# Twenty of eighty expert-score classes in three rounded passes instead of one plain fp32 product, their low parts made by GpSimd

## The chip, the cores and the metric

The kernel runs on one core of a Trainium2 chip. The metric is the device time of one execution in microseconds (us), median over runs. Engine names are those of the profile: PE is the matrix engine (TensorE), PEld its weight loads, DVE VectorE, ACT ScalarE, POOL GpSimd, SP the queue that issues direct DMAs.

## The reference, cut to what matters

The model has two layers. Each ends in a PEER expert block over 256 tokens of width 1024, with 16384 experts:

```
s1, s2 = q[..., :half] . k1, q[..., half:] . k2        # 8 heads, 128 keys each
top 16 of s1, top 16 of s2, top 16 of their 256 sums -> idx, gate = softmax(top)
act = gelu(u_tab[idx] . t)                              # per token, head and choice
out = sum (gate * act) * v_tab[idx]
```

A token picks 8 x 16 of the 16384 experts.

## The kernel before, in words

**Two ways to the experts.** The experts are sorted into 128 classes of 128. For the first `X` = 80 classes the kernel works densely: it computes the scores of all 128 experts of a class for all 256 tokens on PE (80 score classes, "S"), multiplies them by a matrix of gates that is zero where a token has not chosen an expert, and multiplies by the class's rows of `v_tab` (80 value classes, "V"). The other experts are gathered row by row with indirect DMAs issued by POOL and worked on DVE (`gather()`).

**One peer block, in order.** `products()` first makes the queries with `wq` (8 heads, each 2 tiles of 512 KB) in three passes, `mm3`: both factors are split into a rounded high part and a remainder, and high x high, high x low and low x high are added up in one bank. For the weights, ACT makes the high part (a cast into a `whl` tile) and POOL or DVE the low part (a subtraction). For the tokens, `hh` and `hl` (tiles `phh` and `phl`) are high and low, `hf` (`phf`) the plain fp32 values; all three exist before and after the change. Then follow the 80 score classes, 8 fp32 products of 128x256 each, which the profile shows as 16 records, and a Gelu by ACT (`ge<-pa`, later `sg<-pa`). The 80 value classes come last.

**Choosing, at the same time, on DVE.** `choose()` runs `stage2(0)` and `stage2(1)` for the two halves of the tokens: sums of candidates, MAX8/MATCH_REPLACE8/FIND_INDEX8 scans, then long f16 tensor_tensor trees that turn positions into expert numbers. `turn(0)` and `turn(1)` are four PE transposes each (`pa<-identb,ge`) of what a half has chosen. `take8` makes the first lists for the gathers, six memsets prepare the `rows` tiles for gathered rows, and `spread()` builds the gate matrix in 32 blocks: one-hots `o`, `eq` and `oc` on DVE, products `pb<-oc,o` on PE. Three of the six `rows` tiles are the three `whl` buffers, two more are `phl` and `phh`.

**The order.** The kernel's program is written out by a planner: `schedule()` advances the generators of PE work and DVE work by a clock of costs (for PE 0.00167 us a column for a plain fp32 product and 0.00042 for a rounded one), and what is emitted stands in that order on each engine's queue. The chip then follows it in order on every engine, with semaphores between them. The planner's costs know nothing of one engine disturbing another.

**Feeding weights.** `Feed` loads tiles with SP into four `wr` buffers, two or more ahead. A tile with an engine letter is split when it is at most two ahead of its use: the cast goes to ACT's queue, the subtraction for "G" to POOL's. A tile with `None` is used as it is. A `whl` buffer can be filled again when PE has read the tile three before. The bound `feed.hold` stops splitting from the point where `rows` takes the `whl` buffers.

Of the kernel before, what the change touches and what calls it, by code (L numbers as in the profile page):

```python
# [22 lines left out]
KD = 8  # L23
# [2 lines left out]

X = 80
GSC = 32768.0
ROOM = 36
TB, TL = 8, 4  # L30
CAP = 50
# [166 lines left out]
def tile_backbone(ctx: ExitStack, tc: tile.TileContext, a: dict, out: bass.AP):  # L198
# [5 lines left out]
    T, V, S, G, Q = (Engine(e, n, clock) for e, n in ((nc.tensor, "T"), (nc.vector, "V"), (nc.scalar, "S"), (nc.gpsimd, "G"), (nc.sync, "D")))  # L204
# [20 lines left out]
    def pa():  # L225
        t = pp.tile([P, 512], F32, tag="pa", name="pa")
        return t
# [22 lines left out]
    def mm(o, lhsT, rhs, start=True, stop=True):  # L250
        T.matmul(o, lhsT, rhs, start=start, stop=stop)

    def mm3(o, lh, ll, rh, rl, start=True, stop=True):
        T.matmul(o, lh, rh, start=start, stop=False)
        T.matmul(o, lh, rl, start=False, stop=False)
        T.matmul(o, ll, rh, start=False, stop=stop)
# [55 lines left out]
    def x_close():  # L312
        xpool.pop().close()
# [84 lines left out]
    PEER = [(w, c_) for w in "SV" for c_ in range(X)]  # L398
    feed = Feed()
# [5 lines left out]
    for l in range(2):  # L405
        if l:
            feed.add([a["gm_w_v"][n, j] for n in range(4) for j in range(4)] + [a["gm_w_u"][n, j] for n in range(8) for j in range(2)]
                     + [a["gm_w_out"][k] for k in range(16)], GENG)
        feed.add([a["wq"][l, h, j] for h in range(8) for j in range(2)])
        feed.add([a[f"dn{l}"][c_, 0 if w == "S" else 1] for w, c_ in PEER], None)  # L410

    def warm(ps, x):

# [999 lines left out]
    def peer(l, mod, a2, sh2):  # L1413
# [20 lines left out]
        hf = q1.tile([P, KD, 256], F32, name="phf", tag="phf")  # L1434
        hl = q1.tile([P, KD, 256], F32R, name="phl", tag="phl")
        hh = q1.tile([P, KD, 256], F32R, name="phh", tag="phh")
# [20 lines left out]
        def token_major():  # L1457
# [10 lines left out]
            x_close()  # L1468
            qr["s"] = qs = Scratch(ge[:, X - ROOM:, :])
            vals.extend(qs.tile([P, 2, 8, 16], F32, name=f"vals{t}") for t in range(2))  # L1470
# [18 lines left out]
        def stage2(t):  # L1489
# [84 lines left out]
            V.tensor_copy(pk[:, 1, :], i1f)  # L1574
            V.tensor_scalar(pk[:, 2, :], gte[t], GSC, None, op0=ALU.mult)
            V.scalar_tensor_tensor(pk[:, 3, :], gte[t], GSC, pk[:, 2, :], op0=ALU.mult, op1=ALU.subtract)
            yield
# [14 lines left out]
        def turn(t):  # L1592
            pt = pa().bitcast(F16)
            for i in range(4):
                T.transpose(pt[:, i * P:(i + 1) * P], pks[t][:, i, :], identb)
            S.copy(pkT[t], pt[:, :4 * P].rearrange("p (a b) -> p a b", a=4))
# [21 lines left out]
        scored, begun, spreaded = [0], [0], [0]  # L1618

        def spread():  # L1620
# [12 lines left out]
            def apply():  # L1633
                t, b, n, ps, _ = pss.pop(0)
                for i in range(NB):
                    t0 = t * P + b * TB + i * TL
                    v = ps[i][:, :TL * X].rearrange("p (j c) -> p c j", c=X)
                    if n < X:
                        S.activation(ge[:, n:X, t0:t0 + TL], v[:, n:X, :], AF.Copy, scale=1.0 / GSC)
                    o = ge[:, 0:n, t0:t0 + TL]  # L1640
                    V.scalar_tensor_tensor(o, v[:, 0:n, :], 1.0 / GSC, o, op0=ALU.mult, op1=ALU.mult)
                spreaded[0] = t0 + TL
# [31 lines left out]
        def products():  # L1674
            pend = []

            def flush():
                h, qT = pend.pop(0)
                for t in range(2):
                    pss = pa()  # L1680
                    for f in range(2):
                        mm(pss[:, f * P:(f + 1) * P], qT[:, f * 256 + t * P:f * 256 + (t + 1) * P], k12[:, f, h, :])
                    topk1(t, h, pss)

            for h in range(8):
                ps = [pa() for _ in range(2)]
                for j in range(2):
                    wh, wl = feed.get()
                    for f in range(2):
                        for k in range(4):  # L1690
                            mm3(ps[f][:, :256], wh[:, k, f * P:(f + 1) * P], wl[:, k, f * P:(f + 1) * P], hh[:, 4 * j + k, :], hl[:, 4 * j + k, :],
                                j == 0 and k == 0, j == 1 and k == 3)
                if h == 0:
                    token_major()
                qT = qr["s"].tile([P, 512], F32, tag="qT", name="qT", bufs=2)
                for f in range(2):
                    S.copy(qT[:, f * 256:(f + 1) * 256], ps[f][:, :256])
                pend.append((h, qT))
                if h:
                    flush()  # L1700
                yield
            flush()
            done.add("q")

            pair, late = [], []

            def flush_late():

                while late and late[0][0] <= spreaded[0]:
                    _, g_, s_ = late.pop(0)  # L1710
                    V.tensor_tensor(g_, g_, s_, op=ALU.mult)

            for w, c_ in order:
                left[0] -= 1
                if w == "S":
                    u_ = feed.get()
                    ps = pa()
                    for k in range(KD):
                        mm(ps[:, :256], u_[:, k, :], hf[:, k, :], k == 0, k == KD - 1)
                    if len(late) > 2:  # L1720
                        yield lambda: late[0][0] <= spreaded[0]
                        flush_late()
                    n = begun[0]
                    if n:
                        sg = q2.tile([P, 256], F32, tag="sg", name="sg", bufs=4)
                        S.activation(sg[:, :n], ps[:, :n], AF.Gelu)
                    flush_late()
                    if n:
                        late.append((n, ge[:, c_, :n], sg[:, :n]))
                    if n < 256:  # L1730
                        S.activation(ge[:, c_, n:], ps[:, n:256], AF.Gelu)
                    scored[0] += 1
                    if c_ + 1 == X:
                        done.add("S")
                else:
                    while "G" not in done:
                        yield lambda: "G" in done
                    flush_late()
                    if not py[0][0]:
                        for t in range(2):  # L1740
                            for m in range(2):
                                py[t][m] = pb()
                    if c_ == X - 1:
                        done.add("pl")
                    pair.append((ge[:, c_, :], feed.get(2 if c_ >= X - 2 else 1)))
                    if c_ == X - 2:
                        continue
                    for t in range(2):
                        for m, (g_, v_) in enumerate(pair):
                            for n in range(4):  # L1750

                                mm(py[t][n // 2][:, n % 2 * 256:(n % 2 + 1) * 256], g_[:, t * P:(t + 1) * P], v_[:, 2 * n:2 * n + 2, :],
                                   c_ == 0 and n % 2 == 0, c_ == X - 1 and m == 1 and n % 2 == 1 and "shared" in done)
                    pair.clear()
                    done.add("pv")
                    if c_ == 15:
                        done.add("held")
                yield

        def choose():  # L1760
            wait[0], feed.eager = QWAIT, False
            yield lambda: "q" in done
            wait[0] = GTH
            yield from stage2(0)
            for i, _ in enumerate(stage2(1)):
                if i == 4:
                    turn(0)
                yield
            for r_ in range(EARLY):
                take8(0, r_)  # L1770
                yield
            turn(1)
            feed.hold = True
            qr["2"] = eqr.enter_context(tc.tile_pool(name="qr", bufs=2, side="right"))
            qr["rows"] = [whl(f"rows{i}", F32) for i in range(NWH)]
            qr["rows"] += [q1.tile([P, 2 * D], F32, name=f"rows{NWH + i}", tag=("phl", "phh", "row5")[i]) for i in range(NR - NWH)]
            qr["junk"] = qr["2"].tile([P, D], BF16, name="junk", bufs=1)
            for i, r_ in enumerate(qr["rows"]):
                V.memset(r_, 0.0)
            done.add("sel")  # L1780
            todo_v[:] = [order.index(("V", 0)), 2 * P // TB]
            yield from spread()
            done.add("G")
            todo_v[:] = []
            wait[0] = LAST
# [345 lines left out]
```

## Time and profile before

| | |
|---|---|
| runs (3) | median 2077.2 us, 2073.23 to 2078.44 |
| profiled execution | 2073.34 us, of which span 2071.6 us |
| busy in the span | PE 1945.0, PEld 1574.3, DVE 1368.5, ACT 540.4, POOL 592.2 us |
| granted PE clock, mean | 0.973 |
| HBM read | 525.60 MB |

The profile is of one execution. Busy time is the union of an engine's records; a mean duration of a matmul record is longer than the spacing of two, because matmuls overlap. The first score class begins at 520.0 us in layer 0 and at 1409.5 us in layer 1.

### The profile page before, as it was taken

How to read it: one execution, taken by the hardware profiler on the slowest of the kernel's cores; microseconds unless marked ns; L12 is line 12 of the kernel's file. 1: busy time of each engine (PE TensorE's matmuls, PEld its weight loads, DVE VectorE, ACT ScalarE, POOL GpSimd, SP SyncE). 2: the span in 40 equal slices, each digit the busy share in tenths (PEclk: the TensorE clock that was granted, in tenths of full speed). 3: DMA queues.
4: the chain of work that ended last, by engine and by line, in shares of the span. 5: the costliest groups of instructions: out<-in, count | busy, mean ns of one | idle time of the engine just before them, and what ended most of it. 6: DMA issues, size and time to landing. Idle time of an engine off the chain costs nothing.

```text
span 2071.6 us, 28401 instructions
## 1 busy us (share of the span) xinstructions
PE 1945.0 (94%) x10048; PEld 1574.3 (76%) x10048; DVE 1368.5 (66%) x3634; ACT 540.4 (26%) x1386; POOL 592.2 (29%) x378
## 2 busy tenths in 40 slices
PE   7899999999989999998999998999899999989997
PEld 4565444579878888887877788789688888878786
DVE  3575566247988678878664226579888887776651
ACT  4434343344212122210111154442122221101100
POOL 1324222166011112223221188550111112233210
PEclk9999999999989999999999999999999999989999
DMA  8556664555468668998997364454678788989972
GB/s 302 171 184 215 212 217 145 165 173 184 133 225 293 237 220 310 379 378 293 417 410 260 132 234 153 156 191 128 229 283 307 269 297 298 365 295 412 413 274 82
DMA packets 132489, 519.98 MB, mean 251 GB/s; under 512 B 17222, under 2 KB 17414, under 8 KB 107179
## 3 DMA queue, kind: packets, MB, share of 16 engines
q1 hardware_dynamic: 100320, 312.24, 43.2%
q0 software_dynamic: 30720, 204.69, 25.9%
q8 instruction: 79, 1.29, 0.2%
q10 hardware_dynamic: 1296, 1.15, 0.2%
q14 instruction: 74, 0.61, 0.1%
HBM read 525.60 MB, written 6.91 MB: 257 GB/s over the span
## 4 chain that ended last, share of the span: by engine, by line
PE 55%; DVE 19%; issue 12%; DMA 7%; POOL 5%; ACT 2%; POOLq 0%; SPq 0%; ACTq 0%; DVEq 0%
PE pb L169 28%; PE pa L169 27%; DVE ge L169 6%; DMA wr<-in_dn 4%; POOL rows L169 2%; DVE mk L169 2%; POOL whl L169 2%; DVE acc L169 1%; DVE junk L169 1%; DMA acs<-acc 1%; DVE rows L169 1%; DMA rows<-in_uv,gidx 1%; DVE x L169 1%; DVE oc L169 1%; DVE cacc L169 0%
## 5 line engine op out<-in xcount | busy, mean ns | idle before, releaser
L169 PE MATMUL pa<-phf,wr 128*128 128x256 f32 x2560 | 576.1, 386 | 0.0
L169 PE MATMUL pb<-wr,ge 128*128 128x256 f32 x2560 | 569.4, 383 | 6.5 <-DMA wr<-in_dn 5.4
L169 PEld LDWEIGHTS pb<-wr,ge 128*128 128x128 f32 x2560 | 485.2, 191 | 90.3 <-DMA wr<-in_dn 22.9
L169 PEld LDWEIGHTS pa<-phf,wr 128*128 128x128 f32 x2560 | 492.3, 194 | 67.2
L169 POOL DMA_INDIRECT rows<-in_uv,gidx x200 | 231.7, 1158 | 916.8 <-DVE acc L169 608.0
L169 POOL TENSOR_TENSOR whl<-wr,whl 128x1024 fp32r<-128x1024 f32 (+2 forms) x130 | 314.7, 2434 | 401.9 <-ACT whl L169 392.2
L169 DVE SCALAR_TENSOR_TENSOR junk<-rows,h 128x1024 bf16<-128x1024 f32 x200 | 244.0, 1220 | 85.6 <-DMA rows<-in_uv,gidx 82.5
L169 DVE SCALAR_TENSOR_TENSOR acc<-rows,wt,acc 128x1024 f32<-128x1024 f32 x196 | 250.7, 1279 | 0.0
L169 ACT ACTIVATE act<-act 128x1 f32<-128x1 f32 x206 | 41.7, 203 | 435.6 <-DVE junk L169 420.6
L169 ACT CAST whl<-wr 128x1024 fp32r<-128x1024 f32 (+2 forms) x136 | 136.9, 1018 | 70.7 <-PE pa L169 27.7
L169 ACT ACTIVATE sg<-pa 128x256 f32<-128x256 f32 (+25 forms) x126 | 38.8, 308 | 383.9 <-PE pa L169 375.4
L169 PE MATMUL pb<-oc,o 128*128 128x80 f16 x1024 | 88.2, 255 | 31.8 <-DVE oc L169 31.8
L169 PEld LDWEIGHTS <-o 128*128 128x128 f16 x1024 | 80.8, 118 | 40.9 <-DVE o L169 16.3
L169 PE MATMUL pa<-phh,whl 128*128 128x256 f32 x512 | 96.3, 285 | 2.1 <-DVE phf L169 2.1
L169 PE MATMUL pb<-aw,condT 128*32 128x512 f32 x328 | 93.4, 624 | 5.1 <-DVE mod L169 3.0
L169 DVE SCALAR_TENSOR_TENSOR ge<-pb,ge 128x80 f32<-128x80 f32 (+29 forms) x128 | 36.9, 316 | 78.3 <-ACT ge L169 77.2
L169 PEld LDWEIGHTS pa<-phh,whl 128*128 128x128 f32 x512 | 80.8, 191 | 4.0 <-DVE phf L169 2.5
L169 PE MATMUL pa<-phl,whl 128*128 128x256 f32 x256 | 73.2, 286 | 2.4 <-POOL phl L169 1.3
L169 DVE SCALAR_TENSOR_TENSOR mk<-jp,j,gte 128x128 f32<-128x128 f32 x256 | 72.4, 347 | 1.1
L169 PE MATMUL pb<-whl,cath 128*128 128x512 f32 x192 | 61.8, 400 | 2.0 <-POOL whl L169 1.1
L169 ACT ACTIVATE wt<-act,gsel 128x1 f32<-128x1 f32 x200 | 58.9, 295 | 6.5
L169 DVE TENSOR_TENSOR oc<-eq,pkT 128x640 f16<-128x640 f16 x128 | 57.1, 487 | 2.2
(517 smaller groups left out, 2402.0 us busy)
## 6 DMA issues: line engine op xcount, KB each, us to landing
wr<-in_dn SPq DMA_DIRECT2D x320, 512.0 KB
aw<-in_ada_w SPq DMA_DIRECT2D x164, 256.0 KB
wr<-in_wq SPq DMA_DIRECT2D x32, 512.0 KB
wr<-in_w_out SPq DMA_DIRECT2D x16, 512.0 KB
wr<-in_gm_w_v SPq DMA_DIRECT2D x16, 512.0 KB
wr<-in_gm_w_u SPq DMA_DIRECT2D x16, 512.0 KB
wr<-in_gm_w_out SPq DMA_DIRECT2D x16, 512.0 KB
wr<-in_w_xbc SPq DMA_DIRECT2D x12, 512.0 KB
```

The lines of the kernel that those rows point to most:

```text
L169: return f(*args, **kw)
```

## The change

The first `N3` = 20 score classes of each layer are computed with `mm3`, 24 rounded products in place of 8 fp32 ones. Their tiles go through the feed with the letter "G": a cast on ACT and a subtraction on POOL for each. The 60 other classes stay as they are. `choose()` may not pass the point after `turn(1)` before 20 classes are scored in the planner's order.

```diff
+N3 = 20
...
-        feed.add([a[f"dn{l}"][c_, 0 if w == "S" else 1] for w, c_ in PEER], None)
+        feed.add([a[f"dn{l}"][c_, 0] for _, c_ in PEER[:N3]], "G")
+        feed.add([a[f"dn{l}"][c_, 0 if w == "S" else 1] for w, c_ in PEER[N3:]], None)
...
                     for k in range(KD):
-                        mm(ps[:, :256], u_[:, k, :], hf[:, k, :], k == 0, k == KD - 1)
+                        if c_ < N3:
+                            mm3(ps[:, :256], u_[0][:, k, :], u_[1][:, k, :], hh[:, k, :], hl[:, k, :], k == 0, k == KD - 1)
+                        else:
+                            mm(ps[:, :256], u_[:, k, :], hf[:, k, :], k == 0, k == KD - 1)
...
             turn(1)
+            yield lambda: scored[0] >= N3
             feed.hold = True
```

## Rows read from the trace of the kernel before

**Rows 1.** The page: busy times of the engines, and the chain by engine.
```profile
PE 1945.0 (94%) x10048; PEld 1574.3 (76%) x10048; DVE 1368.5 (66%) x3634; ACT 540.4 (26%) x1386; POOL 592.2 (29%) x378
...
PE 55%; DVE 19%; issue 12%; DMA 7%; POOL 5%; ACT 2%; POOLq 0%; SPq 0%; ACTq 0%; DVEq 0%
```

**Rows 2.** Busy time by stretch: length, PE, PEld, DVE, ACT, POOL, clock, DMA.
```profile
519.90:602.70 82.80, 73.93 (x347) 64.36 (x346) 78.39 (x339) 16.57 (x34) 7.46 (x5) 0.96 0.49 164
602.70:800.00 197.30, 189.14 (x1135) 166.38 (x1135) 151.71 (x358) 41.95 (x193) 27.41 (x26) 0.95 0.71 251
...
865.00:1120.00 255.00, 243.47 (x1105) 207.77 (x1104) 187.30 (x466) 31.48 (x125) 76.98 (x63) 0.98 0.95 369
1120.00:1174.00 54.00, 54.00 (x229) 43.02 (x228) 4.26 (x10) 2.37 (x5) 0.00 (x0) 1.00 0.36 119
...
1409.00:1492.00 83.00, 74.32 (x351) 64.75 (x350) 78.58 (x341) 16.93 (x35) 5.57 (x5) 0.97 0.50 164
```

**Rows 3.** PE in order of time, score classes: start, length, records, wait before.
```profile
520.03 34.70 PE L169 MATMUL pa<-phf,wr 128*128 128x256 f32 x160
...
554.79 24.39 PE L169 MATMUL pa<-phf,wr 128*128 128x256 f32 x112
579.37 0.82 PE L169 MATMUL pa<-identb,ge 128*128 128x128 f16 x4 [0.19 <-DVE ge L169]
580.06 14.05 PE L169 MATMUL pa<-phf,wr 128*128 128x256 f32 x64
602.73 0.23 PE L169 MATMUL pb<-oc,o 128*128 128x80 f16 x1 [8.62 <-DVE oc L169]
...
1492.36 0.23 PE L169 MATMUL pb<-oc,o 128*128 128x80 f16 x1 [8.72 <-DVE oc L169]
```

**Rows 4.** PE in order of time, one head of wq in three passes.
```profile
479.49 0.40 PE L169 MATMUL pa<-phh,whl 128*128 128x256 f32 x2
...
485.01 1.06 PE L169 MATMUL pa<-ge 128*128 128x128 f32 x8
```

**Rows 5.** The chain in order of time: DVE's scans of both halves.
```profile
530.23 6.21 DVE ge L169 x40
...
556.36 6.21 DVE ge L169 x40
```

**Rows 6.** DVE by shape, 528.7 to 588.5 us: busy, mean ns, idle before.
```profile
L169 DVE TENSOR_TENSOR ge<-ge,cand 128x2048 f16<-128x2048 f16 x6 | 11.6, 1932 | 0.1
...
L169 DVE TENSOR_TENSOR ge<-ge 128x2048 f16<-128x2048 f16 x4 | 4.9, 1224 | 0.1
L169 DVE SCALAR_TENSOR_TENSOR mk<-jp,j,gte 128x128 f32<-128x128 f32 x16 | 4.5, 348 | 0.1
L169 DVE TENSOR_TENSOR ge<-ge 128x1024 f16<-128x1024 f16 x6 | 4.2, 692 | 0.2
```

**Rows 7.** POOL on weight tiles, 466 to 515 and 1236 to 1272.9 us: ns min/median/max.
```profile
L169 POOL TENSOR_TENSOR whl<-wr,whl x14: 2382/2390/2412, 469.5 to 510.1; 128x1024 fp32r<-128x1024 f32 x14
...
L169 POOL TENSOR_TENSOR whl<-wr,whl x11: 2389/3387/4420, 1236.2 to 1272.9; 128x1024 fp32r<-128x1024 f32 x11
```

**Rows 8.** DVE on the tile gv, 1236 to 1272 us.
```profile
L169 DVE SCALAR_TENSOR_TENSOR junk<-gv x4: 3303/3354/3415, 1236.5 to 1249.7; 128x1024 f32<-128x1024 f32 x4
...
L169 DVE TENSOR_TENSOR gv<-gv,lnb x2: 4342/4344/4346, 1257.6 to 1266.3; 128x2048 f32<-128x2048 f32 x2
```

**Rows 9.** Groups of the whole span by shape: the same DVE form, and ACT's cast.
```profile
L169 DVE SCALAR_TENSOR_TENSOR junk<-rows,h 128x1024 bf16<-128x1024 f32 x200 | 244.0, 1220 | 85.6 <-DMA rows<-in_uv,gidx 82.5 <-issue 2.6 <-DVE acc L169 0.4
L169 ACT CAST whl<-wr 128x1024 fp32r<-128x1024 f32 x120 | 124.1, 1046 | 69.0 <-PE pa L169 26.0 <-issue 22.8 <-PE pb L169 10.1
```

**Rows 10.** ACT in order of time, the exponential of each half.
```profile
536.92 0.31 ACT L169 ACTIVATE gte<-gte 128x128 f32<-128x128 f32 x1 [1.19 <-DVE gte L169]
...
563.05 0.31 ACT L169 ACTIVATE gte<-gte 128x128 f32<-128x128 f32 x1 [2.87 <-DVE gte L169]
```

## The prediction

> **What bounds the kernel now.** I read the page first. PE is busy 94% of the span, and the chain that ended last is 55% PE and 19% DVE [rows 1]: a kernel that PE bounds, with places where DVE sets the pace. Then I cut layer 0's peer block into stretches [rows 2]. From 519.9 to 602.7 us, where experts are chosen, DVE is busy 78.4 of 82.8 us and POOL only 7.5, at its very end. Until 1120 PE is nearly full, and from 1120 to 1174 PE works alone. So the block ends when PE ends; PE time saved early counts unless PE must wait for something that does not move.
>
> PE's own order of time shows what that something is [rows 3]. Records of score classes stand in runs of 160, 112 and 64, at 16 a class: 10 classes, then turn(0), 7 classes, turn(1), 4 classes, then the first product of the spread. There PE waits 8.62 us for oc from DVE (8.72 in layer 1). Turn(1) waited 0.19. The moment 602.7 is thus set by DVE, whatever PE does: 21 classes are done by then, and the 59 others follow.
>
> **The change part by part.**
>
> *PE, cost of a class.* Ten fp32 classes from 520.03 to 554.56 or so take 34.5 us, 3.45 each [rows 3]. In wq's head, three passes run at 46 products from 479.49 to 485.01 [rows 4], 0.120 us each; 24 make 2.88. Saved: 0.57 a class, 11.5 us for 20, 23 us in two layers.
>
> *The planner moves classes.* Its costs are 8 x 256 x 0.00167 = 3.42 us for a plain class and 24 x 256 x 0.00042 = 2.58 for a split one. Its DVE clock is not touched, so the first spread product stands at the same planned time, between 21 x 3.42 = 71.8 and 75.2 us. Twenty split classes take 51.6; the remaining 20.2 to 23.6 hold 6 plain ones. So 26 classes stand ahead of that product instead of 21, and 54 x 3.45 us come after it in place of 59: 17.3 us less PE work behind DVE's moment. (11.5 of this is the passes, the rest is taken out of the 8.6 us wait: PE would reach the product after 20 x 2.88 + 6 x 3.45 = 78.3 us, near 599.) Likewise turn(0) comes after 13 classes or 14, turn(1) after 21 or 22. The new yield asks for 20 and finds them: nothing.
>
> *ACT.* Twenty casts of 1.046 us [rows 9] are 21 us on an engine busy 16.6 of 82.8 [rows 2]: hidden. But they stand in one queue with the exponential of each half, which waits for DVE [rows 10]; when DVE is late, casts behind it are late, then POOL, then PE.
>
> *SP and DMA.* Same bytes and issues; a wr buffer now comes free after POOL's subtraction, earlier than after PE's class. The stretch moves 164 GB/s and later ones 369 [rows 2]. Nothing. The rows tiles that take over whl, phh and phl need class 19 finished; undisturbed that is 520 + 57.6 = 577.6, 11 us ahead of the memsets behind take8, and DVE is later still if disturbed. Nothing.
>
> *POOL.* One subtraction a class: 2.39 us when DVE leaves POOL alone [rows 7], under PE's 2.88. Alone, it would be hidden.
>
> *POOL against DVE.* It is not alone. From 1236 to 1273 us POOL does the same subtraction while DVE normalises: POOL's go from 2.39 to 3.39 and 4.42 [rows 7], and DVE's scalar_tensor_tensor over 1024 fp32 from 1.22 to 3.35 [rows 8, 9]. The excess of each is about the length of the other: POOL 1.0 and 2.0, DVE 2.13. They take turns, one whole instruction each; of the four on DVE none got through in under 3.30. The forms shown with this excess read two operands from SBUF. The choosing stage is made of such forms, 32 in the groups shown alone (11.6 + 4.9 + 4.2 us f16, 4.5 us mk) [rows 6], against the scans, which read one.
>
> The trace before has no POOL subtraction beside an f16 form, so the price is bounded: below, nothing; above, all 20 subtractions at 2.39 us, 47.8 us a layer. I take turns for f16 too, since the nearest rows [rows 8] differ in type alone. The Trainium skill (SBUF — State Buffer, "Who interferes with whom") says that a DVE instruction with two SBUF inputs contends with a GpSimd instruction that reads SBUF, that the later one blocks until the first has finished, and names no type; it speaks against this change. By that rule the sum is the one below; with fp32 forms alone colliding it is that of the first rival.
>
> How many subtractions collide: a subtraction starts some 1.4 us after class c-3 ends (cast 1.05 and two hand-overs, an estimate). Numbers 0 to 3 run before 528.7, during one-input scans of the first top-k. Number 4 meets the sums of candidates; 5 and 6 fall into the scans of 530.2 to 536.4 [rows 5] and are free; from number 7 on DVE is in its trees. PE stops at turn(0) after class 12, so POOL goes on to number 15 and stops too: ten collisions, 4 and 7 to 15. Numbers 16 to 19 follow turn(0); their casts stand behind the second exponential in ACT's queue, which is where the second half's trees begin, so I count four more. Fourteen, at 2.3 us (between the 2.13 and the 2.39), are 32 us that DVE is late at the first spread product, and at the first gather, which stands just ahead of it.
>
> *Sum.* Per layer 32.2 - 17.3 = 14.9 us later; two layers 29.8. Checked on PE's side: it would reach the product at 599 and DVE is there at 602.7 + 32.2 = 634.9, so PE waits about 36 us where it waited 8.8, does 11.5 less work: 27.2 - 11.5 = 15.7. The waits lie at a class in the first trees, at turn(0), at a class behind the second exponential, and at the product; a lowered clock behind the first three is covered by the wait at the last, some 9 us; with that cover gone a few us more. Behind the product the order of DVE, PE and gathers is as before with five classes fewer. 2073.3 + 29.8 = 2103.1 for the profiled execution. The median of the runs lies 3.9 above that execution; I say 2105.
>
> **The rivals.**
>
> *Faster: f16 forms don't take turns with POOL.* Then only the short fp32 forms and mk collide, about three a layer (7 us): 2 x (7 - 17.3) = -20.6, 2053; with none, 2 x -17.3 = -34.6, 2039. For it: no row shows f16 beside a subtraction. Against it: rows 8 show the turn-taking plainly, and f16 reads two operands just the same. The decision lies at 17.3 / 2.3 = 7.5 collisions a layer: fewer, and the kernel is faster.
>
> *No change.* Either about half the subtractions collide, or PE's gain is lost later to DVE's spreads and gathers. For it: PE is short of full by 8.2 us in 602.7 to 800 and by 11.5 in 865 to 1120 [rows 2], where DMA is at 0.95. Against it: 54 us of PE alone at the block's end. 2073 to 2079.
>
> *Worse: all 20 collide, or the planner moves no class ahead.* All 20: 2 x (47.8 - 17.3) = 61, 2134. Fourteen without the moved classes: 64, 2138. Against: the free scans, and the planner's costs.
>
> **How the numbers follow.** My forecast, ten to seventeen collisions, 0.69: 2 x (23 - 17.3) = +11 to 2 x (39.1 - 17.3) = +44, so 2085 to 2120. Faster 0.17, no change 0.08, worse 0.06. One class more or less ahead of the product shifts all by 7 us. The range is 2074 to 2134: it leaves out the faster case (0.17) and half of the worse (0.03). A difference of 0.3% (6 us) is what a measurement of this kernel can tell from none. Slower by more 0.75, within 0.08, faster 0.17.
>
> **What would show it.** In the profile after: the split classes at 2.88 us where PE does not wait (else the first term is wrong); POOL's subtractions from 528 us on at 2.4 plus a DVE form's length, and DVE's f16 trees at their old length plus up to 2.4 (else the main step is wrong); turn(0) waiting some 14 us for DVE; the first oc product near 635 us instead of 602.7, behind 26 classes; the block's last stretch of PE alone as before. If the trees keep their 0.69 and 1.22 us beside POOL, the forecast falls and the first rival holds.

## The result and the profile after

| | before | after |
|---|---|---|
| runs (6 each, same chip) | median 2076.97 us, 2072.95 to 2078.44 | median 2099.36 us, 2092.92 to 2105.49 |
| ratio of the medians | | 1.011, 95% interval 1.0087 to 1.0132 |
| profiled execution, span | 2071.6 us | 2091.2 us |
| granted PE clock, mean | 0.973 | 0.965 |

The change costs 22.4 us by the medians and 19.6 us by the spans of the two profiled executions. The profiled execution of after (2092.92 us) is the lowest of its runs; the balance below is made against spans.

The page of after, busy times and shares of the chain that ended last:

```profile
PE 1937.2 (93%) x10368; PEld 1578.1 (75%) x10368; DVE 1423.2 (68%) x3626; ACT 577.6 (28%) x1430; POOL 703.3 (34%) x418
...
PE 52%; DVE 21%; issue 12%; DMA 8%; POOL 5%; ACT 2%; POOLq 0%; SPq 0%; ACTq 0%; DVEq 0%
```

Against [rows 1] PE is busy for 7.8 us less, although the split classes alone save it 23 us by the prediction's price, and DVE is busy for 54.7 us more (1423.2 - 1368.5), although nothing was added to DVE. That is the first thing to see: another engine's instructions became longer.

PE in order of time, layer 0 (start, length, operation, and in brackets how long PE waited and for whom):

```profile
546.04 0.50 PE L170 MATMUL pa<-phh,whl 128*128 128x256 f32 x2 [2.63 <-POOL whl L170]
...
572.46 0.89 PE L170 MATMUL pa<-identb,ge 128*128 128x128 f16 x4 [10.52 <-DVE ge L170]
...
586.72 0.51 PE L170 MATMUL pa<-phh,whl 128*128 128x256 f32 x2 [2.62 <-POOL whl L170]
...
609.04 0.89 PE L170 MATMUL pa<-identb,ge 128*128 128x128 f16 x4 [2.96 <-DVE ge L170]
609.74 16.62 PE L170 MATMUL pa<-phf,wr 128*128 128x256 f32 x64
...
632.42 0.23 PE L170 MATMUL pb<-oc,o 128*128 128x80 f16 x1 [6.06 <-DVE oc L170]
```

PE stopped for long at one place in [rows 3], the first product of the spread; now it waits for POOL at a class in the first half's trees, for DVE at turn(0), for POOL at a class in the second half's trees, and for DVE at turn(1) and at the first product. That product begins at 632.42 us, 111.0 us after the first score class (its first weight load, 521.41); before it was 602.73, 82.8 us after its first class (519.91). DVE is 28.2 us later there, and 28.5 us in layer 1 (111.5 against 82.95). Ahead of the product stand 25 classes, 20 split and 5 plain, where 21 stood.

DVE's groups by shape in the choosing stage, 528.7 to 618 us (count, busy us, mean ns, idle before):

```profile
L170 DVE TENSOR_TENSOR ge<-ge,cand 128x2048 f16<-128x2048 f16 x6 | 11.6, 1929 | 0.1
L170 DVE TENSOR_TENSOR ge<-ge 128x1024 f16<-128x1024 f16 x6 | 10.4, 1727 | 0.2
L170 DVE TENSOR_TENSOR ge<-ge 128x2048 f16<-128x2048 f16 x4 | 9.0, 2238 | 0.1
L170 DVE TENSOR_TENSOR ge<-ge 128x512 f16<-128x512 f16 x6 | 8.8, 1463 | 0.2
L170 DVE TENSOR_TENSOR ge<-ge 128x256 f16<-128x256 f16 x6 | 6.6, 1100 | 0.2
L170 DVE FIND_INDEX8 ge<-ge 128x8 uint32<-128x50 f32 x32 | 5.8, 203 | 0.0
L170 DVE TENSOR_TENSOR ge<-ge 128x128 f32<-128x128 f16 x4 | 5.8, 1442 | 0.1
...
L170 DVE TENSOR_TENSOR ge<-ge 128x64 f32<-128x64 f32 x4 | 3.1, 771 | 0.0
...
L170 DVE CAST ge<-ge 128x256 f16<-128x256 uint32 x2 | 1.6, 781 | 0.0
```

The shorter forms in before, in the window of [rows 6]:

```profile
L169 DVE TENSOR_TENSOR ge<-ge 128x512 f16<-128x512 f16 x6 | 2.6, 426 | 0.2
L169 DVE TENSOR_TENSOR ge<-ge 128x256 f16<-128x256 f16 x6 | 2.4, 392 | 0.2
...
L169 DVE TENSOR_TENSOR ge<-ge 128x128 f32<-128x128 f16 x4 | 1.6, 391 | 0.1
...
L169 DVE TENSOR_TENSOR ge<-ge 128x64 f32<-128x64 f32 x4 | 0.9, 216 | 0.0
...
L169 DVE CAST ge<-ge 128x256 f16<-128x256 uint32 x2 | 0.6, 278 | 0.0
```

Against [rows 6] the six 128x1024 forms went from a mean of 692 to 1727 ns and the four 128x2048 forms from 1224 to 2238, while the six on `cand` kept theirs (1932 before) because no subtraction met them, and the scans, which read one operand, stayed at 203 ns. POOL's weight tile in the same stage (count, ns min/median/max, first and last start):

```profile
L170 POOL TENSOR_TENSOR whl<-wr,whl x18: 2399/2713/3352, 523.2 to 595.4; 128x1024 fp32r<-128x1024 f32 x18
```

The undisturbed subtraction is 2.4 us as in [rows 7]; the longest is 0.95 us longer. Both sides grow.

The stretches of layer 0 (from : to, length, then busy us and count of PE, PEld, DVE, ACT, POOL, PE clock, DMA share, GB/s), two of after, then the second one of before:

```profile
521.40:632.40 111.00, 85.10 (x571) 80.37 (x570) 106.58 (x339) 34.92 (x56) 56.90 (x23) 0.88 0.42 137
632.40:873.00 240.60, 234.51 (x1392) 207.72 (x1392) 203.16 (x474) 53.43 (x244) 43.50 (x41) 0.98 0.82 299
```

```profile
602.70:865.00 262.30, 254.14 (x1457) 223.81 (x1457) 204.47 (x478) 55.11 (x243) 42.63 (x41) 0.96 0.78 283
```

The choosing stage is longer by 28.2 us with DVE busy in 106.6 of its 111 us, PE in only 85.1, and the granted clock at 0.88. Behind it the stretch up to the first value class (873.01) is shorter: 240.6 us, against 262.2 (602.73 to 864.97).

### The profile page after: what moved, and what is told of

Read it like the earlier page. It is cut to its first block, busy times and chain, and to the rows that moved or that the text cites. A ratio compares the mean times of both kernels' runs of the same rounds, so it can differ in the third digit from the quotient of the medians.

```text
span 2091.2 us, 29147 instructions
## 1 busy us (share of the span) xinstructions
PE 1937.2 (93%) x10368; PEld 1578.1 (75%) x10368; DVE 1423.2 (68%) x3626; ACT 577.6 (28%) x1430; POOL 703.3 (34%) x418
## 4 chain that ended last, share of the span: by engine, by line
PE 52%; DVE 21%; issue 12%; DMA 8%; POOL 5%; ACT 2%; POOLq 0%; SPq 0%; ACTq 0%; DVEq 0%
PE pb L170 29%; PE pa L170 24%; DVE ge L170 9%; DMA wr<-in_dn 6%; POOL rows L170 3%; POOL whl L170 2%; DVE mk L170 2%; DVE acc L170 1%; DVE rows L170 1%; DVE junk L170 1%; DMA rows<-in_uv,gidx 1%; DVE oc L170 1%; DVE x L170 1%; DVE cacc L170 0%; DMA acs<-acc 0%
## 5 line engine op out<-in xcount | busy, mean ns | idle before, releaser
L170 POOL TENSOR_TENSOR whl<-wr,whl 128x1024 fp32r<-128x1024 f32 (+2 forms) x170 | 423.3, 2504 | 462.4 <-ACT whl L170 446.2
L170 PE MATMUL pa<-phf,wr 128*128 128x256 f32 x1920 | 436.9, 388 | 0.0
L170 PEld LDWEIGHTS pa<-phf,wr 128*128 128x128 f32 x1920 | 370.6, 195 | 50.7
L170 PE MATMUL pa<-phh,whl 128*128 128x256 f32 x1152 | 222.8, 293 | 14.5 <-POOL whl L170 10.3
L170 PEld LDWEIGHTS pa<-phh,whl 128*128 128x128 f32 x1152 | 188.7, 200 | 18.0 <-POOL whl L170 11.3
L170 ACT CAST whl<-wr 128x1024 fp32r<-128x1024 f32 (+2 forms) x176 | 178.6, 1024 | 74.7 <-PE pa L170 27.0
L170 PE MATMUL pa<-phl,whl 128*128 128x256 f32 x576 | 167.9, 292 | 2.4 <-POOL phl L170 1.3
L170 PEld LDWEIGHTS pa<-phl,whl 128*128 128x128 f32 x576 | 115.1, 200 | 4.0 <-POOL phl L170 2.1
L170 DVE TENSOR_TENSOR ge<-ge 128x512 f16<-128x512 f16 (+13 forms) x104 | 99.6, 980 | 2.4
L170 DVE SCALAR_TENSOR_TENSOR ge<-pb,ge 128x96 f32<-128x96 f32 (+25 forms) x128 | 38.5, 331 | 62.3 <-ACT ge L170 62.0
```

Of the source, the lines that this page charges most:

```text
L170: return f(*args, **kw)
```

## The experiments

Times are medians; the ratio is to the kernel before, timed beside it (2076.6, 2076.4 and 2077.8 us). "Late" is how much later than in before the first spread product stands after the first score class.

### Is it POOL beside DVE?

The planner's cost for a subtraction on POOL also shifts PE's order a little: after has 25 classes ahead of the product. These four kernels make 20 split classes in one order of PE, with 26 ahead. The first is the control: the planner is not told of the subtraction (`nc.gpsimd` issues it without moving the planner's clock). Here and below, `...` stands for lines left out; the letter that the feed takes for these tiles is changed to match.

```diff
-                    (G if e == "G" else V).tensor_tensor(lo, r, h.bitcast(F32), op=ALU.subtract)
+                    if e == "U":
+                        nc.gpsimd.tensor_tensor(lo, r, h.bitcast(F32), op=ALU.subtract)
+                    else:
+                        (G if e == "G" else V).tensor_tensor(lo, r, h.bitcast(F32), op=ALU.subtract)
```

> The changed kernel with one difference: the planner is not told of the 20 subtractions on GpSimd, so 26 classes stand ahead of the first spread product in place of 25. It is the control for the next three, whose order on TensorE is the same. Turn-taking theory: 14 or so subtractions a layer each hold up one VectorE instruction by about 2.05 us, as in the changed kernel; first spread product about 111 us after the first score class; time 2092 to 2099 us. If the planner's knowledge of GpSimd is what costs (rival), it is near the kernel before, 2077, or under.

Measured: 2099.11 us (2098.47 to 2105.08), ratio 1.0116 [1.0088, 1.0143]; the first product stands 113.2 us after the first class. It behaves as after does, so what it shows of the mechanism holds for after.

Without POOL, the third pass takes the high part again:

```diff
                 S.copy(h, r)
+                if engs == "N":
+                    self.m += 1
+                    h3 = h.rearrange("p (k n) -> p k n", k=kk)
+                    self.out.append((h3, h3))
+                    continue
```

> No low part is made: the third pass takes the high part of the weights again, so the scores of 20 classes are not the reference's. Three passes, the casts on ScalarE and the order on TensorE are those of the control; GpSimd does nothing for these classes. Turn-taking theory: VectorE is not held up, first spread product 82.8 us after the first score class as before the change, with 26 classes ahead of it instead of 21: 2 x 5 x 3.45 = 34.5 us less than before, about 2042 us. Rival (the three passes or the casts standing behind the exponentials cost the time): 2077 or more.

Measured: 2038.37 us (2031.41 to 2044.95), ratio 0.9824 [0.9793, 0.9855]; first product after 83.1 us, 0.3 late. PE in order of time, and the 128x1024 group of DVE (columns as above):

```profile
554.61 0.40 PE L170 MATMUL pa<-identb,ge 128*128 128x128 f16 x4
...
581.96 0.39 PE L170 MATMUL pa<-identb,ge 128*128 128x128 f16 x4
...
600.20 0.23 PE L170 MATMUL pb<-oc,o 128*128 128x80 f16 x1 [3.98 <-DVE oc L170]
```

```profile
L170 DVE TENSOR_TENSOR ge<-ge 128x1024 f16<-128x1024 f16 x6 | 4.2, 692 | 0.2
```

The trees are back at 692 ns, and neither turn waits. Thirteen split classes run from 517.06 to 554.61: 2.89 us each, the prediction's 2.88. So the subtractions on POOL cost 60.7 us (2099.11 - 2038.37); the three passes and the casts by themselves cost nothing, since no_pool is faster than before. The 60.7 us are DVE's lateness: the control's first product stands 30.1 us later in each layer than that of no_pool, and in layer 0 fifteen of its DVE instructions, one more than in after, are longer by 30.3 us in all.

Is it POOL being busy, or POOL reading? Two kernels with the low part made by POOL in other ways, first by two memsets, which only write:

```diff
-                    (G if e == "G" else V).tensor_tensor(lo, r, h.bitcast(F32), op=ALU.subtract)
+                    if e == "W":
+                        G.memset(lo.bitcast(F32), 0.0)
+                        nc.gpsimd.memset(lo.bitcast(F32), 0.0)
+                    else:
+                        (G if e == "G" else V).tensor_tensor(lo, r, h.bitcast(F32), op=ALU.subtract)
```

> The low part is a zero that GpSimd writes by two memsets a tile, so GpSimd is busy for each class and TensorE waits for it, but it reads nothing; the low part of 20 classes is left out of the result. Theory that the two engines take turns at reading: VectorE is not held up, 2042 us like the kernel without GpSimd. Rival 1 (any GpSimd instruction on these tiles holds VectorE up): the product late by 14 times a memset, 2060 to 2095. Rival 2 (the longer chain cast, GpSimd, TensorE is what costs): near the changed kernel.

Measured: 2044.12 us (2041.03 to 2046.98), ratio 0.9842 [0.9816, 0.9868]; 2.2 us late in layer 0. The first of each pair of POOL's memsets, then the same DVE group and two of one-operand forms:

```profile
L170 POOL MEMSET whl<- x19: 951/952/1047, 521.5 to 575.5; 128x1024 f32 x19
...
L170 DVE TENSOR_TENSOR ge<-ge 128x1024 f16<-128x1024 f16 x6 | 4.2, 692 | 0.2
...
L170 DVE TENSOR_SCALAR ge<-ge 128x128 int32<-128x128 int32 x2 | 1.2, 602 | 0.1
L170 DVE COPY ge<-ge 128x8 f16<-128x8 f16 x2 | 1.2, 583 | 0.1
```

Two memsets a tile keep POOL busy for 1.9 us, nearly as long as a subtraction, and DVE's 1024 trees keep their length to the nanosecond. The 2.2 us come from elsewhere: five short one-operand instructions of DVE (a COPY, two CASTs, two TENSOR_SCALARs) ended only when the memset beside them did, up to 0.8 us late; the means of the two groups above were 228 and 186 ns in before. Then by a copy of the raw tile, which reads one operand (a single run, no interval):

```diff
-                    (G if e == "G" else V).tensor_tensor(lo, r, h.bitcast(F32), op=ALU.subtract)
+                    if e == "R":
+                        G.tensor_copy(lo, r)
+                    else:
+                        (G if e == "G" else V).tensor_tensor(lo, r, h.bitcast(F32), op=ALU.subtract)
```

> The low part is a copy of the raw tile by GpSimd, one operand read and one written; the scores of 20 classes are not the reference's. If one read by GpSimd is enough to take turns, each of about 14 copies holds VectorE up by the length of a copy: with 1.2 us the first spread product is 17 us late, 99 us after the first score class, about 2050 us or a little more. If only GpSimd's two-operand instructions take turns: 82.8 us and 2042 us.

Measured: 2054.4 us in its one run; 8.1 us late. POOL's copies and two DVE groups:

```profile
L170 POOL CAST whl<-wr x18: 1041/1054/3175, 520.4 to 576.1; 128x1024 fp32r<-128x1024 f32 x18
...
L170 DVE TENSOR_TENSOR ge<-ge 128x2048 f16<-128x2048 f16 x4 | 7.0, 1762 | 0.1
...
L170 DVE TENSOR_TENSOR ge<-ge 128x1024 f16<-128x1024 f16 x6 | 5.6, 934 | 0.2
```

One read is enough to hold DVE (group means of 1224 to 1762 ns, 692 to 934), by less each time since the copy itself is 1.05 us. DVE was late by 8 us, about half of what I expected: eleven of its instructions were held, by 0.7 us each, not fourteen by 1.2.

### How many subtractions may there be?

The first rival put the turning point at 7.5 collisions a layer. Seven split classes, all with POOL, stay under it, with two or three expected:

```diff
-N3 = 20
+N3 = 7
```

> The change with 7 split classes instead of 20. Their subtractions run before the long trees: two or three collide a layer, 2.5 x 2.05 = 5 us, and 23 classes stand ahead of the first product instead of 21, 6.9 us. Turn-taking theory: 2 x (5 - 6.9) = -4 us, 2073, no measurable change. If a split class cost time in itself, a third of the change's loss: 2085.

Measured: 2077.43 us over 10 runs (2073.48 to 2083.99), ratio 1.0011 [0.9996, 1.0025]: no difference that can be told, with DVE 3.3 us late and 23 classes ahead.

```profile
605.51 0.23 PE L170 MATMUL pb<-oc,o 128*128 128x80 f16 x1 [6.89 <-DVE oc L170]
```

In layer 0 two DVE instructions were held, for 3.2 us in all, so this run does not test the turning point itself. PE still waits 6.9 us for DVE, against 8.6 in [rows 3]. Two classes more ahead (6.9 us) less 3.3 of lateness would win 3.6 us a layer; up to the first value class layer 0 wins 2.3 and layer 1 loses 2.2, with the granted clock behind the product at 0.96 where before had 0.98. Why the clock is lower there is open.

### The low parts on DVE itself

```diff
-  feed.add([a[f"dn{l}"][c_, 0] for _, c_ in PEER[:N3]], "G")
+  feed.add([a[f"dn{l}"][c_, 0] for _, c_ in PEER[:N3]], "V")
```

> The change with the 20 low parts made by VectorE itself, 1.24 us each, 25 us a layer, instead of by GpSimd. The planner knows VectorE's cost and puts 32 classes ahead of the first product. VectorE reaches it near 107 us after the first score class, close to the changed kernel's 111, but TensorE has 20 x 2.88 + 12 x 3.45 = 99 us of work by then. Theory that lateness costs only what TensorE waits: 7 classes more ahead than the changed kernel's 25 are 24 us a layer less behind: about 2045 us. Rival (a late VectorE costs by itself, by late gathers and spreads): as slow as the change, 2095.

Measured: 2049.5 us (2046.56 to 2053.99), ratio 0.9864 [0.9841, 0.9888]. DVE now does the 20 subtractions itself and is 24.7 us late in layer 0, nearly as late as with POOL, and yet the kernel is 49.9 us faster than after. The planner knows DVE's cost, so 32 classes (31 in layer 1) stand ahead of the first product in place of 25: PE has work for the time in which DVE is late. DVE's lateness by itself is not the loss; what is lost is the time for which PE has nothing queued.

### The waits taken away by order alone

If so, moving the planner's DVE clock must pay with no split at all. On the kernel before:

```diff
             turn(1)
+            clk["V"] += 9.0
+            yield
```

> The kernel before, with the planner's VectorE clock put forward by 9 us after turn(1), so that 24 plain classes stand ahead of the first spread product instead of 21; nothing else is changed. It tests the term that a class moved ahead of VectorE's moment is a class saved: 3 x 3.45 = 10.4 us a layer if TensorE's wait of 8.6 us there was the loss, 2 us of it still short, so some 17 us in all: 2060 us. Rival (the wait comes back at later spread products): 2077.

Measured: 2054.69 us (2052.41 to 2056.23), ratio 0.9891 [0.9868, 0.9914]. 24 classes stand ahead; PE at the first product, and the stretch up to it:

```profile
605.21 2.59 PE L169 MATMUL pb<-oc,o 128*128 128x80 f16 x32
```

```profile
520.80:605.20 84.40, 84.08 (x395) 73.44 (x394) 79.95 (x342) 17.68 (x37) 8.48 (x6) 1.00 0.50 169
```

The wait of 8.62 us is gone, PE is busy in 84.1 of 84.4 us, and the granted clock is 1.00. The same on the change, with the clock moved in three places for the lateness seen in after:

```diff
-            yield from stage2(0)
+            for i, _ in enumerate(stage2(0)):
+                if i == 7:
+                    clk["V"] += 20.0
+                yield
             for i, _ in enumerate(stage2(1)):
                 if i == 4:
                     turn(0)
+                if i == 7:
+                    clk["V"] += 11.0
                 yield
...
             turn(1)
+            clk["V"] += 8.0
+            yield
```

> The changed kernel, GpSimd's subtractions and all, with the planner told that VectorE is late: its clock is put forward by 20 us in the first half's trees, 11 in the second's, 8 after turn(1). 37 classes stand ahead of the first product. Turn-taking stays, the product comes 111 to 121 us after the first score class, but TensorE has 20 x 2.88 + 17 x 3.45 = 116 us to do. Theory as above: of the changed kernel's 25 us of waits some 20 a layer go, 2060 us. Rival (late spreads and gathers): behind the product 43 classes are 148 us and the spreads needed 200 us, so TensorE waits there instead: 2080 to 2099.

Measured: 2060.43 us (2060.19 to 2061.33), ratio 0.9923 [0.9901, 0.9945], with 37 classes ahead. The collisions are as before (128x1024 at 1728 ns); 38.9 us came back from order alone. The next limit is the spread:

```profile
832.84 1.37 PE L170 MATMUL pb<-oc,o 128*128 128x80 f16 x16
834.04 6.26 PE L170 MATMUL pb<-wr,ge 128*128 128x256 f32 x28
```

The first value class stands right behind the last spread product (in after, 38 us behind it). DVE's spread now ends where PE's score classes end, so more classes put ahead should gain nothing (not tried). PE comes to the first product 10 us after DVE has its `oc` ready (644.06 against 633.80 us), so a few fewer might do better, which no run tested either. The kernel is still 6 us behind before_later, which splits nothing.

### Splits without collisions, in the right order

> 7 split classes with GpSimd's low parts, and the planner's VectorE clock 9 us forward: 25 classes ahead of the first product, 20.2 + 62.1 = 82.3 us of TensorE work against VectorE's 86. Theory: each term keeps its value when they are put together, 7 x 0.57 = 4 us a layer less than with the clock alone (2054.7), less 1 to 2 us for a later VectorE: about 2049 us. Rival (the gains are the same microseconds): 2055.

```diff
-N3 = 20
+N3 = 7
...
             turn(1)
+            clk["V"] += 9.0
+            yield
```

Measured: 2036.33 us (2035.36 to 2039.17), ratio 0.9802 [0.9784, 0.9819]; 25 classes ahead, the first product with no wait. It came out 13 us better than the sum of its parts as I had worked it out; see the end of the next section.

Fourteen with all their low parts on DVE, the clock not moved:

```diff
-N3 = 20
+N3 = 14
...
-  feed.add([a[f"dn{l}"][c_, 0] for _, c_ in PEER[:N3]], "G")
+  feed.add([a[f"dn{l}"][c_, 0] for _, c_ in PEER[:N3]], "V")
```

> 14 split classes, all low parts by VectorE (17.4 us a layer), clock not moved. 29 classes ahead, 92 us of TensorE work; VectorE arrives at 82.8 + 17.4 = 100, so TensorE waits 8 us as in the kernel before. Theory: 100 + 51 x 3.45 + 41 + 10 = 327 us against 330.5 with the clock alone, about 2048 us. Rival: 2055 or more.

Measured: 2044.52 us (2041.5 to 2045.37), ratio 0.9844 [0.9826, 0.9862], 29 classes ahead, PE's wait at the product down to 2.06 us. And the mixture: five on POOL while DVE scans, nine on DVE, the clock moved:

```diff
-N3 = 20
+N3 = 14
...
-  feed.add([a[f"dn{l}"][c_, 0] for _, c_ in PEER[:N3]], "G")
+  feed.add([a[f"dn{l}"][c_, 0] for _, c_ in PEER[:5]], "G")
+  feed.add([a[f"dn{l}"][c_, 0] for _, c_ in PEER[5:N3]], "V")
...
             turn(1)
+            clk["V"] += 9.0
+            yield
```

> 14 split classes, the low parts of the first 5 made by GpSimd (ahead of the trees, one or two collisions), those of the next 9 by VectorE (11 us), the planner's clock 9 us forward. 30 classes ahead: 14 x 2.88 + 16 x 3.45 = 95.5 us of TensorE work against VectorE's 82.8 + 3 + 11 = 97. Behind the product 50 classes and the spreads, 214 us and some 10 of waits, still longer than the 200 us that the spreads need. Theory: 97 + 224 = 321 us for the score classes of a layer against 330.5 with the clock alone: 2035 to 2042 us, the fastest here. Rival (any VectorE lateness comes back behind the product): 2050 or more.

Measured: 2029.08 us (2026.88 to 2031.18), ratio 0.9772 [0.9754, 0.9789], the fastest here: 48.7 us under before, 70 under after. The low parts by POOL and by DVE, and the stretch up to the first spread product:

```profile
L170 POOL TENSOR_TENSOR whl<-wr,whl x5: 2383/2402/2409, 513.5 to 526.7; 128x1024 fp32r<-128x1024 f32 x5
...
L170 DVE TENSOR_TENSOR whl<-wr,whl x9: 1205/1219/1221, 531.5 to 558.6; 128x1024 fp32r<-128x1024 f32 x9
```

```profile
519.30:618.50 99.20, 96.79 (x604) 89.50 (x603) 91.74 (x352) 31.12 (x55) 15.69 (x9) 1.00 0.53 181
```

None of the five on POOL is longer than 2.41 us, and only one DVE instruction was held by them, a 128x256 cast, for 1.0 us. One on DVE is 1.22 us, half of POOL's 2.4 (group medians). PE is busy in 96.8 of 99.2 us at a clock of 1.00, where after had 85.1 of 111 at 0.88.

## Why the prediction was right, point by point

**The size.** Predicted 2105 us and 29.8 us slower; measured 2099.4 and 22.4 slower (19.6 by the spans). The prediction's own terms, 2073.3 + 29.8 + 3.9, add up to 2107 and not 2105; and its rivals' times stand on the profiled execution of before, not on the median. The forecast case, ten to seventeen collisions, is what happened.

**The cost of a class.** 2.88 us predicted, 2.89 measured where nothing waits (no_pool).

**Turn-taking of POOL and DVE's f16 forms.** Right, and shown: with the same order of PE, subtractions on POOL give 2099, none 2038, write-only instructions 2044. The trace of after agrees with the rule of the Trainium skill that the prediction weighed (SBUF — State Buffer, "Who interferes with whom"): forms with two inputs were held (692 to 1727 ns), scans with one were not (203 ns). The page also says that a GpSimd instruction that only writes does not contend with the two-input forms; pool_writes shows it, at 692 ns. So the first rival (f16 does not take turns) fell. With the subtraction gone the kernel gains 38.2 us over before (no_pool), near the 34.6 that the rival gave for no collision.

**How many, and at what price.** Fourteen DVE instructions were lengthened in each layer, as predicted, but that the number is exact is luck: nine in layer 0 stand ahead of turn(0) and five behind it, where the prediction had ten and four. Subtraction number 4 met a cast and 5 a two-operand form of 128x64, not a scan, and 14 and 15 came behind turn(0), since PE stopped there a class earlier; 14 lengthened nothing. The excesses of the groups, each its busy time less that in before, add up to 28.1 us: 4.1 and 6.2 for the 2048 and 1024 forms, 6.2 and 4.2 for the 512 and 256 forms, 4.2 and 2.2 for the short ones with fp32 output, 1.0 for a cast. That is 2.0 us a collision and not 2.3: the price was the mis-sized term, 28.2 us late (28.5 in layer 1) for 32.2 predicted.

**The moved classes.** In the control, where the planner does not know of the subtraction, turn(0), turn(1) and the first product stand behind 13, 22 and 26 classes, as the prediction worked them out (13 or 14, 21 or 22, 26). In after they stand behind 12, 21 and 25: four classes more than before, 13.8 us (4 x 3.45) and not 17.3. The missing class is due to POOL's planned time, the one thing in which the two kernels differ, and the prediction left it out. The two misses nearly cancel, which is luck: 28.2 - 13.8 = 14.4 a layer, against the 14.9 predicted.

**Where the waits lie.** Ahead of the first product PE waits at the four places named: 2.6 us at a class in the first trees, 10.5 at turn(0) in place of 14, 2.6 at a class behind the second exponential, 6.1 at the product. Turn(1), which the prediction did not name, adds 3.0, and one wait for ACT 1.1: some 26 us, not 36. The rest is a slower clock: PE is busy for 85.1 us with classes that take 75 at 2.88 and 3.45, and the granted clock is 0.88 in that stretch, behind PE's own waits. The prediction had put the clock under the cover of the last wait, and 6.1 us of that wait are left, so it was covered.

**The balance of the spans.** Layer 0 starts 1.5 us later. Then +28.2 up to the first product, -21.6 from there to the first value class (262.2 to 240.6), +0.1 to the end of the block; 2.8 us are won between the layers; in layer 1 +28.5, -13.1 (255.1 to 242.0) and -0.6; behind the last value class -0.5. Together 19.7, the span's 19.6 within rounding. Layer 1 shows the 13.8 of four classes almost alone. Layer 0 wins 7.8 more: the time in which PE is not busy in the stretch behind the product fell from 8.2 to 6.1 us, and PE's busy time fell by 5.8 us beyond the four classes (254.1 to 234.5), with the granted clock at 0.98 in place of 0.96. The prediction said that the order behind the product stays as before and gave this stretch no term but the classes. So the spans' miss of 10 us is mainly this stretch, with the small terms above. The medians miss by 6 only, because after's profiled execution lies 6.4 us under its median and before's 3.6.

**What the prediction did not see.** It took the wait for oc as the place where time is lost and did not ask what the wait itself was worth: before_later removes it, splits nothing, and gains 22 us. In after the planner has not been told that DVE is late by 28 us; told, the change is 39 us faster (change_told), still with all its collisions.

**What stays open.** Seven_told was expected at 2049 and took 2036. Its choosing stages are as expected (86.0 and 87.5 us), but from the first product to the first value class it takes 240.2 and 231.4 us, where before_later takes 246.1 and 247.2 and one class more ahead explains 3.45 of each difference. Most of the rest is in layer 1: PE is busy in 230.1 of the 231.4 us at a granted clock of 1.00, in before_later in 240.9 of 247.2 at 0.97. So it is the clock and fewer waits; why PE waits less there, none of the runs tells.

## What to carry to other kernels

An idle GpSimd is not a free engine: before it gets elementwise work that reads SBUF, look at what DVE does in the same microseconds, and count one turn for every two-operand form that stands there (here 14 turns at 2.0 us, against 11.5 us a layer that the three passes were to save). Put such work beside one-operand scans, or on DVE if DVE does it in half the time, and then tell whoever orders the instructions that DVE is late, so that the engine that waits has work in front of the wait. An engine's wait in the profile before, even a small one at a fixed place, may be worth more than the change that one came to judge.

## What the hardware showed beside this

A DVE CAST with one input from SBUF also took a turn: one of two 128x256 casts grew, and the mean went from 278 to 781 ns. A 128x1024 copy on POOL takes 1.05 us where the subtraction takes 2.4, and held DVE for 8 us in all; one that read nothing (a memset, 0.95 us) held no two-operand tree. But that memset did hold short one-operand COPY, CAST and TENSOR_SCALAR instructions until it ended, up to 0.8 us (pool_writes), while scans with one operand ran at their old length beside the subtraction.
